# Layer 1 of a diffusion-transformer trunk: the latent heads' key, query and value projections moved into the unit loops of neighbourhood and latent attention

## Chip, cores, metric

One core of one Trainium2 chip runs the whole program. The metric is the device time of one execution in microseconds (us). Engines: PE (TensorE) multiplies matrices and transposes, DVE (VectorE) reduces and does elementwise work, ACT (ScalarE) does exp, squares and copies, POOL (GpSimd) does elementwise work in SBUF, SP (SyncE) issues the DMAs. Each engine works through its own queue in order; semaphores hold an instruction back until its inputs are there, and everything queued behind it on that engine waits too.

## Reference, cut to what matters

Two layers over 512 tokens and 256 context tokens, all in float32. Only the mixer of layer 1 is touched:

```python
def mixer_mla_na(h, hc, row, col, ...):
    cq, ckv, kr, nq, nk, nv = split_cols(h @ w_in, sizes)        # also for hc
    # latent heads: 8 heads, 96 = 64 + 32 rotary columns
    mq = rope_tail(rmsnorm((rmsnorm(cq) @ w_uq).reshape(..., 8, 96)))
    kv = (rmsnorm(ckv) @ w_ukv).reshape(..., 8, 64 + 64)
    mk = rope_tail(rmsnorm(concat(kv[..., :64], kr)));  mv = kv[..., 64:]
    o_mla = block_attention(mq, [mkc, mk], [mvc, mv])             # 768 keys
    # neighbourhood heads: 8 heads of 64; window of 8 x 16 columns plus 256 context keys, with a bias
    o_na = neighbourhood_attention(q_na, k_na, v_na, k_nac, v_nac, rpb)
    out = concat([o_mla, o_na]) @ w_out
```

## The kernel before, in words

A float32 product is made of three matmuls (`mm3`): each operand is kept as a high part H and a remainder L. `unit` loads a weight (`wraw`), ACT casts it to H (`wH`), and DVE or POOL subtracts to get L (`wL`).

Layer 1's mixer runs in four stretches. (1) `run_chunks` projects the hidden state: neighbourhood queries, keys, values, and the normalised latents `cq` (384 wide) and `ck` (256 wide). (2) **Neighbourhood attention**: 4 pairs of heads x 4 blocks of 128 queries = 16 *units*. A unit has `scores` (8 matmuls of 256 columns, then softmax: maximum `mc`, bias with maximum, factor `nb` on DVE, two exponentials on ACT, reciprocal `rs` on DVE, scaling of `prob` on POOL), `turn` (8 transposes of `prob` on PE, copied out as `PT` by ACT or DVE), `values` (16 matmuls into `ps_pv`). (3) **Projections of the latent heads**, a `run_chunks` of its own: keys of heads 0 to 3, queries 0 to 3, values 0 to 3, queries 4 to 7, four heads at a time (`two_tiles`). A *make* is the matmuls of two token tiles, then squares on ACT, their sums `ss` on DVE, a reciprocal root on tiles of eight columns (`rsqrt`: `nwm`, `rq` and three rounds of `nwt`, `nwt`, `rq`, all on DVE), the products `qn` and `qr`, for queries a rotation (three products on POOL, one addition on DVE). A *turn* of heads is then 4 transposes on PE for a pair of heads (`turn_pair`) and H and L copied out (`mQH` on ACT, `mQL` on DVE; for keys `mKH`, `mKL`). (4) **Latent attention**: again 16 units, with 12 score matmuls for two heads over 768 keys, 12 transposes, 24 value matmuls; the keys and values of heads 4 to 7 are spread over its first units as background (`more_heads`, `moreq`).

`paired` sets the order of the units on PE: scores of unit u, then the first two groups of transposes of unit u-1, values of unit u-2, background, the rest of the transposes of u-1. `tc.issue_after` pins each block behind the last PE instruction, so PE's order is the one written. The order on DVE, ACT and POOL is chosen when the program is built and is fixed at run time.

Of the kernel before, what the change touches and what calls it, by code (L numbers as in the profile page):

```python
# [28 lines left out]
MLTAB = False  # L29
MKR = 0.8  # L30
EARLY = 3
TAB1 = False
TABR = True
UQ = 4
WS1, NAPT = 4, 6


class Products:


    def __init__(self, engine):
        self.engine, self.last = engine, None

    def matmul(self, *a, **kw):
        self.last = self.engine.matmul(*a, **kw)  # L45
        return self.last

    def transpose(self, *a, **kw):
        self.last = self.engine.transpose(*a, **kw)  # L49
        return self.last  # L50
# [3 lines left out]
def trunk(ctx: ExitStack, tc: tile.TileContext, A: dict, out: bass.AP):  # L54
    nc = tc.nc
    act, dve, pool, pe, sp = nc.scalar, nc.vector, nc.gpsimd, Products(nc.tensor), nc.sync
# [278 lines left out]

    def rope(dst, src, C, S, half, tmp):
# [4 lines left out]
        later(lambda: dve.tensor_tensor(dst, dst, tmp, op=ALU.add), 1)  # L341
# [67 lines left out]
    def paired(units, fill):  # L409
# [5 lines left out]
        def block(f):  # L415
            with tc.issue_after(pe.last.ins):
                f()
# [12 lines left out]
        while True:  # L430
            unit = next(units, None)
            if unit is None and turned is None and valued is None:
                break
            if unit:
                block(unit[0])
            for f in turned[1][:2] if turned else ():
                block(f)
# [3 lines left out]
            for f in turned[1][2:] if turned else ():  # L441
                block(f)
            unit, turned, valued = None, unit, turned
# [514 lines left out]
    with tc.tile_pool(name="g1", bufs=1, side="left") as gp, tc.tile_pool(name="ws1", bufs=1, side="right") as wp:  # L958

        def na_heads(typ, half, tiles, gain, sink):  # L960
# [5 lines left out]
            def compute(units):  # L966
                for t0 in tiles[::2]:
                    pt = (ps_one if t0 < 4 else ps_pv)([P, 512])
# [71 lines left out]
    def kv_units(g, v):  # L1040
        return [unit(A["wukv"][g][:, 512 * v + 256 * i:512 * v + 256 * i + 256], 256, base, tag="c", bufs=KT) for i in range(2)]

    early = []
    mixs = [None] * 8
    with tc.tile_pool(name="atq", bufs=1, side="left") as aq, tc.tile_pool(name="at1", bufs=1, side="left") as ap:
        def low_queries(pr):

            QB = [aq.tile([P, TM], F32R, tag="nQB" + x, name="nQB" + x, bufs=2) for x in "HL"]
            for a, b in zip(QQ[pr], QB):
                both_halves(a, b)  # L1050
            return QB


        QBs = {pr: low_queries(pr) for pr in range(2)}
        V2 = [slot3(F32, name=f"V2{i}")[:, :512] for i in range(3)]
        for i in range(3):
            sp.dma_start(out=V2[i][0:64], in_=V[i][64:128])
            sp.dma_start(out=V2[i][64:128], in_=V[i + 1][0:64])
        base_col = (0, 8, 24, 32)
        wv = ((V[0], V[1]), (V2[0], V2[1]), (V2[1], V2[2]), (V[2], V[3]))  # L1060

        def na_units(pr):
            mixs[4 + pr] = group_pair(0, "mix")
            if pr == EARLY:
                early.extend([kv_units(0, 0)])
            pvs = {}
            QB = QBs.pop(pr) if pr in QBs else low_queries(pr)

            bias = {}
            for hd in range(2):  # L1070
                for i, b in enumerate((0, 1, 3)):
                    bias[hd, b] = base.tile([P, TC], F32, tag="c" + "HL"[hd], name="bias", bufs=KT)
                    sp.dma_start(out=bias[hd, b], in_=A["bias"][2 * pr + hd, i])
                    pool.tensor_scalar(bias[hd, b], bias[hd, b], 8.0, 1.0, op0=ALU.mult, op1=ALU.mult)
                bias[hd, 2] = bias[hd, 1]
            for b in range(4):
                tq = slice(128 * b, 128 * b + 128)
                st = {}

                def scores(b=b, tq=tq, st=st):  # L1080
                    wk = slice(8 * base_col[b], 8 * base_col[b] + 256)
                    st["p"] = [ap.tile([P, 512], F32, tag="P", name="prob", bufs=5) for _ in range(2)]
                    for hd in range(2):
                        S = ps_one([P, 512])
                        (QH, QL), K = (QQ[pr], QB)[hd], (KA, KB)[hd][pr]
                        for so, ko in ((slice(0, 256), wk), (slice(256, 512), CTX)):
                            pe.matmul(S[:, so], QH[:, tq], K[:, ko], start=True, stop=False)
                            last = pe.matmul(S[:, so], QL[:, tq], K[:, ko], start=False, stop=True)
                        mc = small.tile([P, 2], F32, tag="mc", name="mc")
                        mx = small.tile([P, 2], F32, tag="mx", name="mx")  # L1090
                        dve.reduce_max(mc[:, 0:1], S[:, 256:512], axis=AX)
# [360 lines left out]
```

## Time and profile before

| | |
|---|---|
| three timed runs | median 1741.58 us (1740.38 to 1742.42) |
| the profiled execution | 1739.45 us, span 1737.7 us |
| busy over the span | PE 1655.2 us (95%), DVE 942.6 (54%), ACT 631.0 (36%), POOL 251.8 (14%) |
| chain that ended last | PE 87%, DVE 6%, ACT 3%, POOL 2% |

The span runs from the first to the last instruction; 1.8 us of the execution lie outside it. The profile also gives, for each stretch, the clock that PE was granted as a share of 2.4 GHz (1.2 GHz is 0.5). Matmuls overlap, so that a "busy" PE may still be fed slowly; the spacing of starts tells more.

### The profile page before, as it was taken

Reading aid. Unit: us, or ns where it says so; the run is one execution under the profiler, and the core shown is the slowest. Engines: PE = TensorE matmul, PEld = TensorE weight load, DVE = VectorE, ACT = ScalarE, POOL = GpSimd, SP = SyncE. Lnnn points to the kernel's source line nnn. Section 1 sums busy time; section 2 is a strip of 40 time slices with the busy share of each in tenths; the row PEclk is TensorE's granted clock in tenths of the full one; section 3 lists DMA queues with packets and bytes.
Section 4 is the critical chain, followed back from the end, with each engine's and each line's share of the span. In section 5 each row is a group of like instructions: output and inputs, shape, how many; then the busy total and the mean of one; then the engine's idle time right before and its main releaser. Section 6 shows DMA issues by size and latency. Waiting matters only on the chain.

```text
span 1737.7 us, 28925 instructions
## 1 busy us (share of the span) xinstructions
PE 1655.2 (95%) x11590; PEld 1469.8 (85%) x11590; DVE 942.6 (54%) x2052; ACT 631.0 (36%) x1217; POOL 251.8 (14%) x440
## 2 busy tenths in 40 slices
PE   6898999999999999999999999777999999999999
PEld 3688677788888888888889999666789998999897
DVE  5687567555845524433326874568866633333332
ACT  4454556524221221221224643454554432232221
POOL 1341333211000000000001202455330100000000
PEclk8899999999999999999999999897999999999999
DMA  7401334311635513522212223302003132222221
GB/s 280 156 35 53 137 131 171 131 39 54 210 102 175 171 56 134 170 70 65 70 64 100 79 70 97 91 15 76 25 25 134 40 109 96 85 98 98 98 77 58
DMA packets 60662, 171.23 MB, mean 99 GB/s; under 512 B 7152, under 2 KB 14576, under 8 KB 60528
## 3 DMA queue, kind: packets, MB, share of 16 engines
q1 hardware_dynamic: 60528, 169.39, 29.0%
q8 instruction: 91, 1.49, 0.3%
q14 instruction: 43, 0.35, 0.1%
HBM read 160.05 MB, written 4.19 MB: 95 GB/s over the span
## 4 chain that ended last, share of the span: by engine, by line
PE 87%; DVE 6%; ACT 3%; POOL 2%; DMA 1%; issue 1%; SPq 0%; POOLq 0%; ACTq 0%; DVEq 0%
PE ps_one L45 52%; PE ps_tp L45 15%; PE ps_pv L45 9%; PE ps_big L45 7%; PE ps_tp L49 5%; ACT prob L395 1%; POOL prob L399 1%; DVE mx L390 0%; DVE wL L144 0%; DVE win L648 0%; DVE ss L350 0%; ACT wH L143 0%; DVE rq L269 0%; DVE qn L598 0%; DVE nwt L267 0%
## 5 line engine op out<-in xcount | busy, mean ns | idle before, releaser
L143 ACT CAST wH<-wraw 128x1024 fp32r<-128x1024 f32 (+5 forms) x209 | 194.3, 937 | 390.9 <-PE ps_one L45 209.6
L144 DVE TENSOR_TENSOR wL<-wraw,wH 128x1024 fp32r<-128x1024 f32 (+4 forms) x199 | 222.9, 1125 | 172.2 <-ACT wH L143 170.0
L45 PE MATMUL ps_one<-hH,wL 128*128 128x512 f32 (+1 forms) x704 | 236.8, 336 | 0.0
L45 PE MATMUL ps_one<-hL,wH 128*128 128x512 f32 (+1 forms) x704 | 236.7, 336 | 0.0
L45 PE MATMUL ps_one<-hH,wH 128*128 128x512 f32 (+1 forms) x704 | 236.7, 336 | 0.0
L45 PE MATMUL ps_tp<-hH,wL 128*128 128x256 f32 x704 | 196.6, 280 | 0.0
L45 PE MATMUL ps_tp<-hL,wH 128*128 128x256 f32 x704 | 196.3, 279 | 0.0
L45 PE MATMUL ps_tp<-hH,wH 128*128 128x256 f32 x704 | 196.0, 280 | 0.0
L45 PE MATMUL ps_one<-aH,wL 128*128 128x512 f32 (+1 forms) x560 | 194.0, 347 | 0.0
L45 PE MATMUL ps_one<-aL,wH 128*128 128x512 f32 (+1 forms) x560 | 193.9, 347 | 0.0
L45 PE MATMUL ps_one<-aH,wH 128*128 128x512 f32 (+1 forms) x560 | 193.5, 347 | 0.0
L309 POOL TENSOR_SCALAR hH<-nt 128x256 fp32r<-128x256 f32 (+1 forms) x72 | 39.5, 557 | 736.6 <-ACT nt L308 734.6
L45 PEld LDWEIGHTS ps_one<-hH,wL 128*128 128x128 f32 x704 | 132.2, 188 | 15.4
L45 PEld LDWEIGHTS ps_one<-hL,wH 128*128 128x128 f32 x704 | 132.2, 188 | 14.4
L45 PEld LDWEIGHTS ps_one<-hH,wH 128*128 128x128 f32 x704 | 132.3, 188 | 14.2
L399 POOL TENSOR_SCALAR prob<-prob,rs 128x768 f32<-128x768 f32 (+2 forms) x136 | 105.2, 782 | 195.7 <-DVE rs L397 157.0
L45 PEld LDWEIGHTS ps_tp<-hH,wH 128*128 128x128 f32 x704 | 132.3, 188 | 0.9
L45 PEld LDWEIGHTS ps_tp<-hL,wH 128*128 128x128 f32 x704 | 132.0, 188 | 1.0
L45 PEld LDWEIGHTS ps_tp<-hH,wL 128*128 128x128 f32 x704 | 132.2, 188 | 0.1
L49 PE MATMUL ps_tp<-ident,prob 128*128 128x128 f32 x656 | 99.5, 285 | 20.6 <-POOL prob L399 18.0
L45 PEld LDWEIGHTS ps_one<-aH,wH 128*128 128x128 f32 x560 | 105.8, 189 | 14.7
L45 PEld LDWEIGHTS ps_one<-aL,wH 128*128 128x128 f32 x560 | 105.6, 189 | 14.5
(274 smaller groups left out, 3456.3 us busy)
## 6 DMA issues: line engine op xcount, KB each, us to landing
wraw<-in_ada_dram SPq DMA_DIRECT2D x80, 512.0 KB, 3.7
wraw<-in_wg_dram SPq DMA_DIRECT2D x44, 512.0 KB, 3.5
wraw<-in_wu_dram SPq DMA_DIRECT2D x44, 512.0 KB, 3.5
wraw<-in_wd_dram SPq DMA_DIRECT2D x32, 384.0 KB, 3.1
wraw<-in_wd_dram SPq DMA_DIRECT2D x16, 512.0 KB, 3.5
wraw<-in_w1n_dram SPq DMA_DIRECT2D x12, 512.0 KB, 3.4
adaw<-in_adaq_dram SPq DMA_DIRECT2D x16, 256.0 KB, 5.4
wraw<-in_adaq_dram SPq DMA_DIRECT2D x8, 512.0 KB, 5.6
```

The lines of the kernel that those rows point to most:

```text
L45: self.last = self.engine.matmul(*a, **kw)
L49: self.last = self.engine.transpose(*a, **kw)
L143: act.copy(H, raw[:, :cols])
L144: eng.tensor_tensor(L, raw[:, :cols], H.bitcast(F32), op=ALU.subtract)
L309: last = (pool.tensor_scalar(H, t[:, :n], 1.0, 1.0, op0=ALU.mult, op1=ALU.mult), sub(L, t[:, :n], H))
L395: act.activation(pr[i], S[:, i, :], AF.Exp, bias=nb[:, i:i + 1], scale=scale, accum_out=sm[:, i:i + 1])
L399: pool.tensor_scalar(pr[i], pr[i], r[:, i:i + 1], 1.0, op0=ALU.mult, op1=ALU.mult)
```

## The change

Stretch (3) is gone. Its makes and turns become small closures that are listed, unit by unit, in `na_plan` and `mla_plan`; `paired` runs the closures of a unit between the values and the transposes. Both attentions are one sequence of 32 units on the same score, probability and `PT` buffers, with no drain between them. Queries are made two heads at a time (192 columns instead of 384), so there are 8 query makes instead of 4, each with its own reciprocal root. In neighbourhood units the softmax of both heads is joint (one `mc`, one `nb`, one `rs`), and all transposes of a unit come after values and background (0 early groups, 2 before). The zero rows of queries and keys are written once per buffer over all tokens. The `wL` of the key and value weights moves from DVE to POOL, and the addition of the rotation stands right behind its products.

```diff
+    def padded(pair):
+        for x in pair:
+            pool.memset(x[96:128, :].bitcast(F32), 0.0)
+        return pair
...
+    def query_steps(pr, w):
...
+        def make(t0):
+            if t0 == 0:
+                mQ[2 * pr:2 * pr + 2] = [padded(group_pair(0, "mQ") if pr < 2 else mQx[2 * pr - 4 + i]) for i in range(2)]
+                st["w"] = w()
+            pt = ps_pv([P, 2, 256])
+            for i in range(2):
+                tok_gemm(pt[:, i, :192], st["w"], 1, 192, lq[t0 + i])
+            o = st[t0] = raw_heads(2)
+            hv = pt[:, :, :192].rearrange("p t (h d) -> p t h d", d=96)
+            r = tile_rstd(hv, o)
...
+            dve.tensor_tensor(qn, hv[..., 64:96], bc(r, [P, 2, 2, 32], 3), op=ALU.mult)
+            dve.tensor_tensor(o[..., 0:64], hv[..., 0:64], bc(r, [P, 2, 2, 64], 3), op=ALU.mult)
...
+            rope(o[..., 64:96], qn, C, S, 16, tmp, now=True)
+
+        def turn(t0):
+            turn_pair(t0, st[t0], gcol["mqg"], mQ[2 * pr:2 * pr + 2])
+
+        return [f for t0 in (0, 2) for f in ((lambda t0=t0: make(t0)), (lambda t0=t0: turn(t0)))]
...
             background()
-            for f in turned[1][2:] if turned else ():
+            for f in unit[4] if unit else ():
                 block(f)
-            unit, turned, valued = None, unit, turned
+            for f in turned[1][early:] if turned else ():
+                block(f)
+            turned, valued = unit, turned
...
+                dve.reduce_max(mc, S[:, :, 256:512], axis=AX)
...
+                softmax(S, 2, 512, 0.125, st["p"], mx)
...
+    na_plan = [q[0][:1], q[0][1:2], q[0][2:3], q[0][3:], q[1][:1], q[1][1:2], q[1][2:3], q[1][3:],
+               keys0[0][:1], keys0[0][1:2], turns0[0][:1], keys0[0][2:], turns0[0][1:2], turns0[0][2:] + [v0], [], []]
+    mla_plan = [vals0[:2], vals0[2:] + turns0[1][:1] + [hq[0]], turns0[1][1:] + [k1], q[2][:1],
+                q[2][1:2] + keys1[0][:1], q[2][2:3] + turns1[0][:1], q[2][3:] + keys1[0][1:2] + [v1, hq[1]], keys1[0][2:] + turns1[0][1:],
+                vals1[:2], vals1[2:] + q[3][:1], q[3][1:3] + turns1[1][:1], q[3][3:] + turns1[1][1:],
+                [], [], [], []]
...
-        paired((u for pr in range(4) for u in mla_units(pr)), [(moreq, 2 * MKR)])
+    uq0()
+    k0()
+    paired(both_attentions())
```

On DVE, a neighbourhood unit before had its two heads one after the other, and the next unit's maxima between them (`mc`: maximum over the context scores; ISA: bias and maximum; `rs`: reciprocal of the exponentials' sum):

```order
L1091 TENSOR_REDUCE mc<-ps_one 128x1
L1092 ISA ps_one,mx<-ps_one,bias,mc 128x256
L1092 ISA mx 128x1
L1091 TENSOR_REDUCE mc<-ps_one 128x1
L392 TENSOR_SCALAR nb<-mx 128x1
L1092 ISA ps_one,mx<-ps_one,bias,mc 128x256
L1092 ISA mx 128x1
L392 TENSOR_SCALAR nb<-mx 128x1
L144 TENSOR_TENSOR wL<-wraw,wH 128x256
L397 RECIPROCAL rs<-sm 128x1
L1091 TENSOR_REDUCE mc<-ps_one 128x1 x2
```

In the change, with a query make (here the first) beside units 0 and 1, the same engine has:

```order
L375 TENSOR_SCALAR nb<-mx 128x2
L380 RECIPROCAL rs<-sm 128x2
L1090 TENSOR_REDUCE ss<-qr 128x4
L238 TENSOR_SCALAR nwm<-ss 128x4
L244 TENSOR_SCALAR rq<-nwm 128x4
L247 SCALAR_TENSOR_TENSOR nwt<-rq 128x4
L1212 TENSOR_REDUCE mc<-ps_big 128x2
...
L1143 TENSOR_TENSOR qn<-ps_pv,rq 128x128
L1144 TENSOR_TENSOR qr<-ps_pv,rq 128x4x64
L380 RECIPROCAL rs<-sm 128x2
L322 TENSOR_TENSOR qr<-qr,rt 128x4x32
L345 SCALAR_TENSOR_TENSOR mQL<-ps_tp,par,mQH 96x256 x2
```

`rs` of the even unit now stands directly behind its `nb`, the make's sums behind that, the odd unit's maximum behind these, and the rotation's addition (L322) behind the odd unit's `rs`.

On PE, the block between two units' scores of the neighbourhood loop was transposes and values alone; in the change the first turn of queries (L1080) stands behind the scores of unit 1 and ahead of the transposes of unit 0's probabilities:

```order
L1211 MATMUL ps_big<-nKB,nQBL 128x256
L1080 MATMUL ps_tp<-ident,qr 96x128 x4
L389 MATMUL ps_tp<-ident,prob 128x128 x8
L1210 MATMUL ps_big<-nKA,nQH_9220 128x256
```

The make of these queries stands one unit earlier. In the latent loop (unit 4) the turn stands behind the values and ahead of a key make and of unit 3's last transposes:

```order
L1270 MATMUL ps_pv<-PT,mV_9195 64x128 x2
L1080 MATMUL ps_tp<-ident,qr 96x128 x4
L135 MATMUL ps_pv<-wH,ck_9201 128x256
L136 MATMUL ps_pv<-wL,ck_9201 128x256
L137 MATMUL ps_pv<-wH,ck_9202 128x256
...
L389 MATMUL ps_tp<-ident,prob 128x128 x4
L135 MATMUL ps_big<-mKH,mQH 128x512
```

Before, these transposes belonged to stretch (3), where no attention unit was queued behind them.

## Rows read from the trace of the kernel before

**Rows 1.** The page, part 2: PE busy and granted clock, 40 slices, in tenths.
```profile
PE   6898999999999999999999999777999999999999
PEclk8899999999999999999999999897999999999999
```
**Rows 2.** Windows: the four stretches; busy us (count) by engine, PE clock, DMA.
```profile
1089.20:1163.20 74.00, 56.34 (x512) 47.03 (x512) 43.80 (x179) 39.05 (x94) 33.62 (x73) 0.93 0.20 51
1163.20:1213.90 50.70, 35.58 (x206) 33.06 (x203) 40.92 (x135) 22.69 (x53) 32.27 (x90) 0.79 0.21 71
1213.90:1267.90 54.00, 50.20 (x422) 44.00 (x421) 41.41 (x114) 29.67 (x65) 15.28 (x21) 0.97 0.12 38
1267.90:1315.00 47.10, 46.64 (x456) 40.50 (x454) 29.16 (x67) 24.43 (x52) 15.97 (x18) 1.00 0.01 4
```
**Rows 3.** Timeline of PE, a neighbourhood unit without stalls (start, us, instruction).
```profile
1108.20 0.39 PE L45 MATMUL ps_one<-nKA,nQH 128*128 128x256 f32 x1
...
1109.25 1.03 PE L49 MATMUL ps_tp<-ident,prob 128*128 128x128 f32 x8
...
1111.24 0.39 PE L45 MATMUL ps_one<-nKA,nQH 128*128 128x256 f32 x1
```
**Rows 4.** Timeline of PE: the first work after three gaps (gap in brackets).
```profile
1095.57 1.11 PE L49 MATMUL ps_tp<-ident,prob 128*128 128x128 f32 x4 [4.35 <-POOL prob L399]
1124.72 1.92 PE L49 MATMUL ps_tp<-ident,prob 128*128 128x128 f32 x8 [2.80 <-POOL prob L399]
1190.66 0.69 PE L45 MATMUL ps_big<-wH,cq 128*128 128x384 f32 x1 [3.94 <-DVE qr L1167]
```
**Rows 5.** Groups by form, 1087 to 1320 us: softmax and rotation (busy us, mean ns).
```profile
L1092 DVE CUSTOM_DVE_ANT_0 ps_one<-ps_one,bias,mc 128x256 f32<-128x256 f32 x32 | 15.2, 485 | 0.3
L395 ACT ACTIVATE prob<-ps_one,nb 128x512 f32<-128x512 f32 x32 | 21.8, 688 | 7.5 <-DVE nb L392 7.3
L395 ACT ACTIVATION_READ_ACCUMULATOR prob<-ps_one,nb 128x1 f32 x32 | 6.4, 201 | 0.0
L399 POOL TENSOR_SCALAR prob<-prob,rs 128x512 f32<-128x512 f32 x32 | 21.9, 692 | 21.9 <-DVE rs L397 11.1 <-PE ps_one L45 4.9 <-DVE nb L392 4.2
L340 POOL TENSOR_TENSOR qr<-qn,tab1q 128x128 f32<-128x128 f32 x8 | 3.7, 467 | 0.0
```
**Rows 6.** Groups by form on DVE, 1164 to 1214 us: makes and turns.
```profile
L1149 DVE TENSOR_REDUCE ss<-qr 128x8 f32<-128x512 f32 x3 | 2.1, 688 | 2.4 <-ACT qr L1147 2.4
L267 DVE SCALAR_TENSOR_TENSOR nwt<-rq 128x8 f32<-128x8 f32 x21 | 5.8, 284 | 0.3
L268 DVE TENSOR_TENSOR nwt<-nwt,nwm 128x8 f32<-128x8 f32 x21 | 3.8, 187 | 0.4
L269 DVE SCALAR_TENSOR_TENSOR rq<-nwt,rq 128x8 f32<-128x8 f32 x21 | 5.0, 246 | 0.4
L362 DVE SCALAR_TENSOR_TENSOR mQL<-ps_tp,par,mQH 96x256 fp32r<-96x256 f32 x12 | 5.5, 474 | 0.2
```
**Rows 7.** Timeline, latent unit 2 beside a key make: PE's scores, PE's next turn, DVE's sums and last root step.
```profile
1227.84 0.48 PE L45 MATMUL ps_big<-mKH,mQH 128*128 128x512 f32 x1
...
1232.47 0.64 PE L49 MATMUL ps_tp<-ident,qr 128*96 128x128 f32 x4
...
1228.73 0.68 DVE L1149 TENSOR_REDUCE ss<-qr 128x8 f32<-128x512 f32 x1
...
1235.08 0.17 DVE L269 SCALAR_TENSOR_TENSOR rq<-nwt,rq 128x8 f32<-128x8 f32 x1
```
**Rows 8.** Timeline of PE: a key make up to its turn, and two latent units without background.
```profile
1246.09 0.39 PE L45 MATMUL ps_pv<-wH,ck 128*128 128x256 f32 x1
...
1247.61 0.60 PE L49 MATMUL ps_tp<-ident,qr 128*96 128x128 f32 x4
...
1273.11 0.48 PE L45 MATMUL ps_big<-mKH,mQH 128*128 128x512 f32 x1
...
1278.13 0.47 PE L45 MATMUL ps_big<-mKH,mQH 128*128 128x512 f32 x1
```

More of the change, by code (lines that the diff above doesn't have):

```diff
@@ L407, in transposed, with paired @@
         copy_out(dst, tp[:, :128 * n].rearrange("p (a b) -> p a b", a=n), acts, of)
-    def paired(units, fill):
+    def paired(units, fill=()):
         debt = [0.0] * len(fill)
         def block(f):
-            with tc.issue_after(pe.last.ins):
+            last = next(i for i in reversed(nc.cur_bb.bb.instructions) if i.engine == mybir.EngineType.PE)
+            with tc.issue_after(last):
                 f()
@@ new lines, in value_steps, with make, once, get @@
+    def value_steps(g, w):
+        def make(t0):
+            pt = ps_pv([P, 2, 256])
+            for i in range(2):
+                tok_gemm(pt[:, i, :], w(), 1, 256, lk[t0 + i])
+            for i in range(2):
+                act.copy(mV[t0 + i][:, 256 * g:256 * g + 256], pt[:, i, :])
+        return [lambda t0=t0: make(t0) for t0 in (0, 2, 4)]
+    def once(f):
+        got = []
+        def get():
+            if not got:
+                got.append(f())
+            return got[0]
+        return get
@@ new lines, in trunk, with mla_units, scores, turn @@
+    wo1 = [[]]
+    def mla_units(pr, plan):
+        pvs = {}
+        if pr == 3:
+            for i in range(4):
+                wo1[0] += cut(unit(A["w1o"][0][:, 256 * i:256 * i + 256], 256, base, tag="c", bufs=KT, eng=pool), 2)
+        for t in range(4):
+            tq = slice(128 * t, 128 * t + 128)
+            st = {}
+            def scores(tq=tq, st=st):
+                st["p"] = [ap.tile([P, TT], F32, tag="P", name="prob", bufs=4) for _ in range(2)]
+                for hd in range(2):
+                    (QH, QL), (KH, KL_) = mQ[2 * pr + hd], mK[2 * pr + hd]
+                    S = ps_big([P, 1024])
+                    for ko in (MAIN, CTX):
+                        mm3(S[:, ko], (QH[:, tq], QL[:, tq]), (KH[:, ko], KL_[:, ko]), True, True)
+                    softmax(S[:, :TT].unsqueeze(1), 1, TT, 96 ** -0.5, [st["p"][hd]])
+            def turn(i, st=st):
+                if i == 0:
+                    st["t"] = ap.tile([P, 12, 128], F32, tag="PT", name="PT", bufs=2)
+                transposed([st["p"][j // 6][:, 128 * (j % 6):128 * (j % 6) + 128] for j in range(4 * i, 4 * i + 4)],
+                           st["t"][:, 4 * i:4 * i + 4, :])
+            def values(t=t, tq=tq, st=st):
+                if t == 0:
+                    pvs["pv"] = ps_pv([P, 512])
+                for kt in range(6):
+                    for hd in range(2):
+                        h = 2 * pr + hd
+                        pe.matmul(pvs["pv"][64 * hd:64 * hd + 64, tq], mV[kt][:, 64 * h:64 * h + 64],
+                                  st["t"][:, 6 * hd + kt, :], start=kt == 0, stop=kt == 5)
+                if t == 3:
+                    mixs[pr] = group_pair(0, "mix")
+                    put_pair(pvs["pv"], 512, mixs[pr])
+            yield scores, [lambda i=i, turn=turn: turn(i) for i in range(3)], values, 2, plan[t]
@@ new lines, in both_attentions @@
+    def both_attentions():
+        nonlocal mKx, mQx
+        for pr in range(4):
+            yield from na_units(pr, na_plan[4 * pr:4 * pr + 4])
+        wqs.close()
+        aqs.close()
+        na.close()
+        mp = mla.enter_context(tc.tile_pool(name="mla", bufs=1, side="left"))
+        mQx = [tuple(mp.tile([P, TM], F32R, tag=f"mQ{x}{i}", name=f"mQ{x}{i}") for x in "HL") for i in range(4)]
+        mKx = [mp.tile([P, TT], F32R, tag=f"mKx{i}", name=f"mKx{i}") for i in range(4)]
+        for pr in range(4):
+            yield from mla_units(pr, mla_plan[4 * pr:4 * pr + 4])
```

334 lines of the change are left out of this document (130 added, 204 removed).

## The prediction, made before the changed kernel was timed

> **What bounds the kernel now.** I read the page's slices first [rows 1]. PE is busy nine tenths or more nearly everywhere; only slices 26 to 28 show 7, and there the granted clock falls too. That is layer 1's mixer, so I cut it into its stretches with the windows view [rows 2]: 74.0 us neighbourhood attention, 50.7 us projections of the latent heads, 54.0 us latent attention with background and 47.1 us without, 225.8 us in all. PE is busy 56.3 of 74.0 and 35.6 of 50.7 us in the first two, against 50.2 of 54.0 and 46.6 of 47.1 in the others. At the same time DVE is busy 40.9 of 50.7 us in the projections (81%) and 43.8 of 74.0 (59%) in neighbourhood attention. So two engines matter: PE has 38 us without work in the whole, DVE has 70.
>
> Then the timeline. A neighbourhood unit without stalls takes PE 3.04 us [rows 3], so that 16 take 48.7 of the 74 us. A latent unit without background takes 5.02 us [rows 8], 16 take 80.3. A key make takes 1.52 us [rows 8]; its turn half a microsecond. With 6 key and 6 value makes, queries worth about 16 us and 20 turns, PE's work in the 225.8 us is about 173 us at full clock. Moving the projections into the units could therefore gain up to 50 us, if nothing but PE counted. What decides is whether DVE can deliver each make in the time that PE needs to come to its turn.
>
> **The change, part by part.** *Query units of neighbourhood attention (units 0 to 7).* A make and its turn stand in alternate units. I lay out two units from the end of an even unit's scores, in DVE's order as shown with the change. The joint maximum over 2 x 256 costs what a sum over 512 costs, 0.69 [rows 6]; two bias passes at 0.485 [rows 5], their accumulators and `nb` bring it to 2.0 us. Two exponentials with their accumulator, 2 x 0.69 + 0.2 less a small overlap [rows 5], end at 3.5. `rs` waits for both, and DVE has nothing ahead of it: 1.5 us idle. Then `ss` (0.55 for 384 elements, between nothing and the 0.69), the odd unit's maximum after its scores, bias and `nb` with the first root steps in between: 7.9. PE has meanwhile done values 1.0, the next make 2.0, transposes 1.0, scores 1.05 and values 1.0, and has nothing left from 6.9. The remaining five root steps at some 0.2 [rows 6], `qn` and `qr` end at 9.6; the rotation's three POOL products, each at most 0.47 [rows 5], end at 10.45, its addition at 10.8. Only now the turn can start; the 8 transposes of the even unit and the next scores are queued behind it on PE. Turn 0.5, transposes 1.0, scores 1.05: 13.4 us for two units, with a stall of 4 us in it. Before, two units took 2 x 74.0/16 = 9.25.
>
> The first pair takes longer, about 19: the query weights' `wL` and eight new zero fills stand on POOL ahead of the first probabilities, and PE waits for the weights. The zero fills (32 x 512 and 32 x 768) have no row; I bound one by nothing and by a whole `prob` pass of 0.69 [rows 5], 0 to 5.5 us for eight, and take half, which the first softmax mostly hides; with no cover it is 3 us. The 192-column matmul has no row either: between nothing and the 0.127 us of a key make's twelve [rows 8], 0 to 2.3 us a make; I take 2.0, near the upper row, the nearest there is. So units 0 to 7 take 19 + 3 x 13.4 = 59 us at full clock.
>
> *Units 8 to 15* carry three key makes and three turns, the last two nothing. A key turn comes two units after its make, so PE does not wait for it; DVE sets the pace. Its work is 8 x 2.4 for softmax and `PT`, 3 x 3.6 for makes (sums, nine root steps at 0.24 [rows 6], products), 6 x 0.47 for `mKL` [rows 6], 0.7 for the mix: 33.5, and some 1 us a unit waiting for exponentials in the units that have nothing to fill it: 39 us.
>
> *Latent units.* PE's work is 80.3 + 4 query makes x 2.0 + 9 key or value makes x 1.5 + 13 turns x 0.5 = 108. Here the trace shows the chain itself [rows 7]: scores start at 1227.84, the make's sums at 1228.73, and its last root step, threaded between two heads' maxima, ends at 1235.25, 7.4 us after the scores began. Less one `mKL` that stood in between, that is 7.0; with `qn`, the rotation and its addition, 8.75 us after the scores began. PE comes to the turn 4.63 us after them (1232.47, [rows 7]). Before, that was the turn of an earlier make; now it is this one's, so PE waits 4.1 us. This holds for units 4, 6 and 10. In unit 11 the sums start earlier: 2.7. In unit 7 a key make is followed by its own turn: squares, sums, nine steps and product, 5.0. With 1 us for unit 5 the stalls are 21 us, and the latent units take 129 us against 101.1 before.
>
> *What a stall costs besides.* After gaps of 2.8 to 4.35 us PE runs at its lower level, 1.2 GHz: eight transposes took 1.92 us at 1124.72 [rows 4] against 1.03 [rows 3], and the first 384-column matmul after 3.94 us took 0.69 [rows 4]; stretch 3 had a mean clock of 0.79 [rows 2]. Behind each new stall stand a turn, transposes and scores, 2.5 us of PE work that would double. Eight stalls cost 0 to 20 us; I take 9, since a slower PE also finds DVE further ahead. The Trainium skill (TensorE: Matmul & The Clock Gate, section "HAM oscillation — how this bites in real kernels") says that waits between groups of matmuls can send the clock back to its lower level group after group, so that each begins slow; by that the whole 20 would be paid, and [rows 4] agree for the gaps named.
>
> *Free parts.* `wL` on POOL: POOL is busy 33.6 of 74 us [rows 2], and the units that get them have spare POOL time. Later queue positions of DMAs on SP: DMA engines are 20% busy there [rows 2]; uncovered, one late weight is one transfer of some 3 us. The boundary without drain saves about 2 us of waiting, which is in the sum, since I count units straight through.
>
> **Sum.** First scores 1.0; units 0 to 7 59 + 4 of the clock's 9; units 8 to 15 39; latent units 129 + 5; less 2.1, since units 0 to 15 were counted to the end of unit 16's scores: 235 us against 225.8. That is +9 on the profiled execution's 1739.45, so 1748.5; the runs' median stands 2.1 above that execution. I forecast **1749 us**. Ends: query units 54 to 70, the next 35 to 41, latent 120 to 142: 209 to 252 us, -17 to +26, hence 1724 to 1767.
>
> **Rivals.**
> *Faster.* The turn's chain on DVE is shorter than I lay it out, because softmax work and root steps fill each other's gaps, and PE comes to the turns when they are ready. For it: DVE has 70 us without work in the stretch, and held 81% through stretch 3 [rows 2]. Its work grows by four roots, 4 x 9 x 0.24 = 8.6, to 164 us; at 81% that takes 202, a gain of 23: 1718; halfway between that and no change, 1730. Against it: order on DVE is fixed, and [rows 7] show 7 us. It decides at latent unit 4: a wait under 2 us there means this case.
> *No change.* PE fills neighbourhood attention's gaps and gives the same back at the turns: eight stalls of 2.5 instead of 4 us take 12 off the sum and leave 223: 1739. The change then moves the idle time and does not shorten it.
> *Clock in full.* Every stall pays the lower level, +11: 1760. Stretch 3 ran so; against it, PE is fed better between the stalls here.
>
> **How the numbers follow.** Forecast (own range 1745 to 1757) 0.43, faster 0.31, no change 0.20, clock in full 0.06. A difference of 0.2%, 3.5 us, is about what a measurement of this kernel can tell from none. So slower 0.49, same 0.20, faster 0.31. The range takes in most of the faster case and the upper bound: 1722 to 1764.
>
> **What would show it.** In the profile after: stretch 3 gone; eight neighbourhood units in about 60 us, where before eight took 37; waits of PE of some 4 us at the turn of queries, released by DVE's or ACT's work on `qr`; PE clock below 0.95 through the first 100 us; DVE near 75% busy. Wrong would be: PE's longest waits at the turns under 2 us, or no waits but a clock near 1.

## The result and the profile after

The changed kernel takes 1798.91 us (median of 4 runs, 1798.47 to 1800.78) against 1741.66 of the kernel before on the same chips: ratio 1.0332, interval [1.0314, 1.0349]. It is slower by 57 us. Forecast were 1749 and a range of 1722 to 1764: the sign was right, the size was not. All the time is lost in layer 1's mixer: from the first scores of neighbourhood attention to the first feed-forward matmul behind it the trace of before has 272.3 us (1089.2 to 1361.5), that of after 331.1 (1089.3 to 1420.4).

The page of after, part 2, against [rows 1]:

```profile
PE   6897999999999999999999996678679999999999
PEclk8898999999999999999999997799889999999999
```

Windows of after: units 0 to 7, units 8 to 15, latent units 0 to 11, each from scores to scores (us; busy us and count of PE, its weight loads, DVE, ACT, POOL; clock, DMA share, GB/s).

```profile
1089.26:1162.81 73.55, 44.20 (x306) 39.42 (x305) 37.11 (x130) 25.56 (x59) 27.81 (x52) 0.72 0.20 51
1162.81:1208.70 45.89, 35.70 (x306) 31.06 (x305) 31.72 (x111) 22.05 (x55) 18.38 (x31) 0.89 0.05 15
1208.70:1341.37 132.67, 98.78 (x792) 87.67 (x790) 77.49 (x222) 57.26 (x127) 44.45 (x69) 0.89 0.10 31
```

The low stretch has not gone, as a kernel without stretch 3 should show: it has grown from three slices to six. In units 0 to 7 PE works 44 of 73.6 us, at a clock of 0.72, and no other engine is busy for more than 37.1. That is the picture of a chain of waits, not of a full engine. Lines of the view of waits, after, 1089 to 1366 us, name it (us in total, times, longest):

```profile
PE ps_tp L1080 <- DVE qr L322: 40.3, 8, 6.3
PE ps_tp L389 <- ACT PT L165: 6.0, 5, 2.9
PE ps_pv L135 <- DVE qr L1111: 5.4, 3, 3.3
PE ps_tp L1080 <- POOL qr L1113: 5.0, 1, 5.0
DVE qr L322 <- POOL qr L320: 9.0, 8, 2.0
```

All eight query turns (L1080) wait for the rotation's addition (L322), 5.0 us in the mean; unit 7's key turn waits as long. One of them in order of time, units 2 and 3 (start, us, instruction, idle time before):

```profile
1111.57 0.36 PE L135 MATMUL ps_pv<-wH,cq 128*128 128x192 f32 x1
...
1114.45 0.55 DVE L1090 TENSOR_REDUCE ss<-qr 128x4 f32<-128x384 f32 x1 [0.56 <-ACT qr L1087]
1114.91 1.37 POOL L382 TENSOR_SCALAR prob<-prob,rs 128x512 f32<-128x512 f32 x2
1115.04 0.60 DVE L238 TENSOR_SCALAR nwm<-ss 128x4 f32<-128x4 f32 x1
...
1116.42 0.69 DVE L1212 TENSOR_REDUCE mc<-ps_big 128x2 f32<-128x512 f32 x1
...
1119.58 0.41 DVE L1144 TENSOR_TENSOR qr<-ps_pv,rq 128x256 f32<-128x256 f32 x1
...
1120.85 0.78 DVE L322 TENSOR_TENSOR qr<-qr,rt 128x128 f32<-128x128 f32 x1 [0.60 <-POOL qr L320]
1121.77 1.06 PE L1080 MATMUL ps_tp<-ident,qr 128*96 128x128 f32 x4 [5.11 <-DVE qr L322]
...
1124.60 1.09 PE L389 MATMUL ps_tp<-ident,prob 128*128 128x128 f32 x4 [0.91 <-DVE PT L167]
```

The make starts at 1111.57, its sums at 1114.45; the next unit's maximum (1116.42) stands between its root steps, the product starts at 1119.58, the rotated half is there at 1121.6, and PE, out of work at 1116.7, begins the turn at 1121.77. Then turn, transposes and scores run at the lower clock level: the turn took 1.06 us against 0.60 in [rows 8]. The window from this turn to the end of unit 4's scores, in the columns of the windows above:

```profile
1121.77:1127.38 5.61, 4.70 (x22) 4.08 (x23) 1.50 (x3) 1.53 (x3) 1.22 (x3) 0.50 0.05 18
```

The granted clock was 0.50 (1.2 GHz) in all of it. In the 2.5 us behind each of the eight query turns it was 0.50 seven times and 0.57 once. In the two pairs with the longest waits (6.27 and 6.14 us, units 5 and 7) POOL adds to the chain: it scales both heads' probabilities first, though `qn` is ready. Unit 5:

```profile
1137.12 0.27 DVE L1143 TENSOR_TENSOR qn<-ps_pv,rq 128x128 f32<-128x128 f32 x1
1137.37 1.36 POOL L382 TENSOR_SCALAR prob<-prob,rs 128x512 f32<-128x512 f32 x2 [3.92 <-DVE rs L380]
1138.69 0.32 POOL L318 TENSOR_TENSOR rt<-qn,tab1q 128x64 f32<-128x64 f32 x1
```

### The profile page after: what moved, and what is told of

It reads as the page before. It is cut to its first block, busy times and chain, and to the rows that moved or that the text cites. A ratio compares the mean times of both kernels' runs of the same rounds, so it can differ in the third digit from the quotient of the medians.

```text
span 1796.7 us, 29025 instructions
## 1 busy us (share of the span) xinstructions
PE 1674.8 (93%) x11662; PEld 1488.7 (83%) x11662; DVE 949.9 (53%) x2052; ACT 633.7 (35%) x1224; POOL 256.1 (14%) x403
## 4 chain that ended last, share of the span: by engine, by line
PE 84%; DVE 7%; ACT 3%; POOL 2%; issue 1%; DMA 1%; SPq 0%; ACTq 0%; POOLq 0%; DVEq 0%
PE ps_one L136 16%; PE ps_one L135 16%; PE ps_one L137 16%; PE ps_tp L137 5%; PE ps_tp L135 5%; PE ps_tp L136 5%; PE ps_tp L389 4%; PE ps_pv L777 2%; PE ps_pv L135 2%; PE ps_pv L136 1%; PE ps_pv L137 1%; PE ps_big L135 1%; PE ps_big L136 1%; PE ps_big L137 1%; ACT prob L378 1%
## 5 line engine op out<-in xcount | busy, mean ns | idle before, releaser
L123 ACT CAST wH<-wraw 128x1024 fp32r<-128x1024 f32 (+6 forms) x212 | 194.4, 926 | 393.0 <-PE ps_one L136 194.5
L124 DVE TENSOR_TENSOR wL<-wraw,wH 128x1024 fp32r<-128x1024 f32 (+3 forms) x191 | 219.6, 1155 | 169.2 <-ACT wH L123 167.3
L378 ACT ACTIVATE prob<-ps_big,nb 128x768 f32<-128x768 f32 (+2 forms) x136 | 104.5, 775 | 48.1 <-DVE nb L375 33.2
L135 PEld LDWEIGHTS ps_one<-aH,wH 128*128 128x128 f32 x560 | 105.8, 189 | 14.7
```

Source lines behind the costliest of these rows:

```text
L123: act.copy(H, raw[:, :cols])
L124: eng.tensor_tensor(L, raw[:, :cols], H.bitcast(F32), op=ALU.subtract)
L135: pe.matmul(o, aH, bH, start=first, stop=False)
L378: act.activation(pr[i], S[:, i, :], AF.Exp, bias=nb[:, i:i + 1], scale=scale, accum_out=sm[:, i:i + 1])
```

## The experiments

The theory (own make): a query turn stands one unit behind its make, the make's chain over ACT, DVE and POOL is longer than PE's work up to the turn, and everything behind the turn in PE's queue waits with it. Rivals: the new form of neighbourhood attention's softmax (both heads at once) makes the units long; the half clock behind the waits; POOL's zero fills; the number of PSUM buffers; DVE's total work. Times are medians, ratios are to the kernel before, timed beside each run. The split by stretches stands in a table behind the ninth run; it is that of the one profiled execution of each kernel.

**Run 1: turns two units behind their makes in neighbourhood attention.**

```diff
-    na_plan = [q[0][:1], q[0][1:2], q[0][2:3], q[0][3:], q[1][:1], q[1][1:2], ...
+    na_plan = [q[0][:1], q[0][2:3], q[0][1:2], q[0][3:], q[1][:1], q[1][2:3], ...
```

> One change to the kernel after: in the eight units of neighbourhood attention that carry queries, each turn stands two units behind its make (make, make, turn, turn) instead of one. Own-make theory (a query turn waits on PE for the DVE chain of a make that is one unit old, and everything behind it on PE waits too): the four waits there of 5.1 to 6.3 us, 22.9 in sum, and the half clock behind them go; units 0 to 7 fall from 73.6 to about 50 us and the whole from 1799 to about 1775. Softmax-form theory (the joint softmax of two heads with all transposes behind the background makes the units long): the units keep 65 us or more and the whole stays above 1790.

Measured: 1785.34 us, 1.0264 [1.0246, 1.0282]. Units 0 to 7 fell from 73.6 to 55.2 us, as the own-make theory has it and the softmax theory does not; but units 8 to 15 rose from 45.9 to 52.8, so that 13.6 us remain of the 24 expected. Two of the four waits are left, 3.5 and 3.6 us at units 3 and 7.

**Run 2: the same in the latent units too.**

```diff
-  ... turns0[1][1:] + [k1], q[2][:1], q[2][1:2] + keys1[0][:1], q[2][2:3] + turns1[0][:1], ...
+  ... turns0[1][1:] + [k1] + q[2][:1], keys1[0][:1], q[2][1:2] + q[2][2:3], keys1[0][1:2] + turns1[0][:1], ...
```

> As the run before, and in the latent units too every query turn and unit 7's key turn stand at least two units behind their make. Own-make theory: the latent waits at query turns (17.3 us), at unit 7's key turn (5.0) and at its make (3.3) go as well, with the half clock behind them (about 10): some 30 us less than the run before, about 1743, near the kernel before. Softmax-form theory: latent units were not changed in form, so the latent part may gain, but the neighbourhood part stays above 110 us for its 16 units, and the whole above 1765.

Measured: 1775.47 us, 1.0201 [1.0184, 1.0218]. The latent units 0 to 11 gave 12.5 of the 30 us expected. PE's waits in this run, 1089 to 1343 us, show why:

```profile
PE ps_pv L135 <- DVE qr L1144: 7.8, 3, 2.8
PE ps_pv L135 <- DVE qr L1111: 7.5, 3, 2.9
PE ps_tp L1080 <- DVE qr L322: 7.2, 3, 3.5
PE ps_tp L389 <- POOL prob L382: 6.0, 1, 6.0
```

The turns' waits fell from 40.3 to 7.2 us, but in their place the next make now waits for the product of the make ahead of it (L1144 and L1111, 15.3 us): of the two `ps_pv` buffers the values' accumulator holds one, and each make keeps the other until the end of its chain. And a wait of 6.0 us for POOL is new. So the own-make wait is a true cause, and the PSUM wait stood behind it; where the wait for POOL comes from, run 3 shows.

**Run 3: PE computes through the wait.**

```diff
         tp = ps_tp([P, 2, 256])
+        for _ in range(fill):
+            pe.matmul(tp.rearrange("p a b -> p (a b)"), ckH[:, 0, 0:128], ckH[:, 0, 0:512], start=True, stop=True)
```

`fill` is 16 for query turns and 0 for key turns.

> The kernel after, with 16 matmuls of 512 columns on data that is always there, written into the query turn's own result tile ahead of its transposes (they are overwritten), so that PE computes through its wait. Some 3.8 us of matmuls at full clock, for a wait of 4 to 6 us. Clock theory (a good part of the loss is the half clock after each wait): eight turns with 2.5 us each of work that no longer doubles, 15 to 25 us less, 1775 to 1785. Own-make theory alone, with the clock as a small part: within 6 us of 1799, since the chain on DVE is as long as before.

Measured: 1796.22 us, 1.0321 [1.0305, 1.0336]; 2.7 us less than after, with intervals that overlap. Yet units 0 to 7 took 66.0 us instead of 73.6, at a mean clock of 0.90 instead of 0.72, and units 8 to 15 took 7.2 us more, with one wait of 6.75 us in them. Behind unit 3's turn the clock was back:

```profile
1119.91:1124.00 4.09, 3.21 (x32) 2.88 (x34) 2.09 (x4) 1.50 (x3) 1.31 (x3) 1.00 0.13 37
```

The clock theory holds locally, 7.5 us for four waits in these units and 3 in the latent ones, about half of what it expected, and the whole does not show it, because something else took it back. It is on POOL. First after, then this run (the last row is PE's):

```profile
1205.19 1.36 POOL L382 TENSOR_SCALAR prob<-prob,rs 128x512 f32<-128x512 f32 x2 [2.08 <-DVE rs L380]
...
1207.29 0.73 POOL L1067 MEMSET mKL<- 32x768 f32 x1
```

```profile
1199.16 0.73 POOL L1067 MEMSET mKL<- 32x768 f32 x1 [1.80 <-PE ps_big L1213]
...
1204.27 2.77 POOL L1067 MEMSET mKx<- 32x768 f32 x4
1207.14 1.36 POOL L382 TENSOR_SCALAR prob<-prob,rs 128x512 f32<-128x512 f32 x2
...
1207.89 1.97 PE L389 MATMUL ps_tp<-ident,prob 128*128 128x128 f32 x8 [6.75 <-POOL prob L382]
```

In after the last neighbourhood unit's probabilities stand ahead of the zero fills of the latent queries and keys on POOL; in this run the build has put them behind the fills, 8 us of them, and PE waits. The same wait, 6.0 to 8.0 us, stands in runs 1 to 4, 8 and 9: in each run that keeps the fills. So each of these six has a cost in units 8 to 15 that comes from POOL's order and not from what it tests.

**Run 4: background behind the transposes of the unit before** (in `paired`, the two loops that issue `unit[4]` and the remaining transposes change places).

> The kernel after, with a unit's background issued behind the transposes of the unit before instead of ahead of them; plan and distances of turns as they are. Own-make theory: each turn comes on PE one block of eight transposes later (1 to 2 us), so eight waits of 5 shrink by that much and the probabilities' transposes no longer stand behind them, 10 to 20 us less: 1780 to 1790. If it were not the place of the turn in PE's queue that counts but DVE's total work: no change, 1797 to 1801. Against a gain: makes come later too, and DVE gets their sums later, which could give all of it back.

Measured: 1797.90 us, 1.0330 [1.0304, 1.0355]. Units 0 to 7 gave 7.0 us, units 8 to 15 took 6.0 back with the fills' wait (8.0 us here). In the whole, no change, which is the number of the rival. The step expected is not what gave the 7.0 us: the four turn waits of units 0 to 7 hardly shrank, 21.7 us against 22.9.

**Runs 5 and 6: no zero fills, on after and on run 2.**

```diff
-        for x in pair:
-            pool.memset(x[96:128, :].bitcast(F32), 0.0)
...
-                        mm3(S[:, ko], (QH[:, tq], QL[:, tq]), (KH[:, ko], KL_[:, ko]), True, True)
+                        mm3(S[:, ko], (QH[:96, tq], QL[:96, tq]), (KH[:96, ko], KL_[:96, ko]), True, True)
```

> The kernel after without POOL's 32 zero fills of rows 96 to 127: the latent scores contract over the 96 rows that hold data instead of 128, with the same result. Zero-fill theory (the fills, 0.52 to 0.73 us each and 20 us in all, stand in POOL's queue ahead of the probabilities' passes and of the keys' products): at least 8 us less, 1791 or below, most of it in the first two units and at units 14 to 17. Own-make theory: PE's waits at the query turns end with DVE's addition and not with POOL's fills, so within 4 us of 1799.

> The same edit on top of the run with all turns late (1775.5), where PE waited 6.0 us for the last neighbourhood unit's probabilities while POOL worked through twelve fills. Zero-fill theory: that wait falls under 2 us and units 14 to 17 give 6 to 10 us with the clock, 1765 to 1770. If the fills only stand where POOL would wait for something else anyway: 1773 to 1777.

Measured: 1801.53 us, 1.0345 [1.0325, 1.0365] on after, so the fills cost after nothing; 1769.10 us, 1.0155 [1.0131, 1.0178] on run 2, 6.4 us less, as the zero-fill theory has it: units 0 to 7 from 54.5 to 47.7 and units 8 to 15 from 52.7 to 47.1, while the latent units 0 to 11 took 4.7 more. The fills are a cost in waiting: hidden as long as something slower stands ahead, and paid as soon as that is removed.

**Run 7: makes copy their product out of PSUM at once, on run 6.**

```diff
+            act.copy(o, hv)
...
-            dve.tensor_tensor(o[..., 0:64], hv[..., 0:64], bc(r, [P, 2, 2, 64], 3), op=ALU.mult)
+            dve.tensor_tensor(o[..., 0:64], o[..., 0:64], bc(r, [P, 2, 2, 64], 3), op=ALU.mult)
```

The edit also moves `qn` and `rt`, which had one buffer each, into the tile of their make; no run separates the two.

> On top of the run before: each query and key make copies its product from PSUM to SBUF on ACT at once and DVE takes the products from that copy, so that the PSUM buffer comes free after two ACT operations and not with the last product of the chain, some 8 us later. PSUM theory (of two buffers the values hold one, so a make cannot begin before the make ahead of it has gone through its whole chain on DVE; with late turns this wait took the turn's place, 15.3 us in six waits): the six waits go, the latent units 3 to 11 fall from about 10 to about 8 us each, 15 to 22 us less than the run before. Rival, DVE's order sets the pace (a unit with a make and a turn has 8 us of work on DVE plus waits for exponentials): PE then waits elsewhere, for the turns again, and less than 6 us are gained.

Measured: 1747.86 us, 1.0034 [1.0023, 1.0045]: 21 us less than run 6, at the upper end of the PSUM theory. The latent units 0 to 11 fell from 123.7 to 104.0 us, and waits of PE for L1144 and L1111 at `ps_pv` are gone. The Trainium skill (Perfetto Trace Analysis, section "Optimization Strategy") says that the same gap coming back on the engine that should be full can mean too few buffers for the next tile. Run 2's six waits of 2.3 to 2.9 us are such gaps, and run 7 bears it out.

**Run 8: neighbourhood attention's softmax head by head, on after.**

```diff
-                dve.reduce_max(mc, S[:, :, 256:512], axis=AX)
...
-                softmax(S, 2, 512, 0.125, st["p"], mx)
+                for hd in range(2):
+                    dve.reduce_max(mc[:, hd:hd + 1], S[:, hd, 256:512], axis=AX)
...
+                    softmax(S[:, hd:hd + 1, :], 1, 512, 0.125, [st["p"][hd]], mx[:, hd:hd + 1])
```

> The kernel after with one part undone: neighbourhood attention's softmax head by head (maximum, bias pass, exponential and division of one head after the other, as before the change) in place of both heads together; all else as in after. Softmax-form theory: each of the 16 units has its first exponential 1.2 us earlier and is 0.5 to 1 us shorter, 1785 to 1791. Own-make theory: two more small operations a unit on DVE stand in the chain of the make, so no gain, 1797 to 1805.

Measured: 1802.16 us, 1.0349 [1.0324, 1.0373]. Units 0 to 7 took 74.3 us against 73.6, so there is no gain there. Units 8 to 15 took 50.4 against 45.9 with the fills' wait in them (7.6 us), so that this run can't tell for them; run 16 does.

**Run 9: run 7's copy alone, on after.**

> The kernel after with the early copy from PSUM alone; turns one unit behind their makes and the zero fills as in after. If the two causes stand in a row (first the turn waits for its own make, and only with that gone does the next make wait for the PSUM buffer): PE still waits 4 to 6 us at eight query turns, the buffer is not what ends these waits, and little is gained, 1792 to 1801. If the buffer alone were the cause and the late turns only moved work: 1775 or less.

Measured: 1812.30 us, 1.0404 [1.0388, 1.0420]; 13 us slower than after, beyond both expectations. PE's waits, 1085 to 1380 us:

```profile
PE ps_tp L1080 <- DVE qr L322: 42.5, 8, 7.2
PE ps_tp L1080 <- POOL qr L1115: 11.2, 3, 4.8
PE ps_tp L389 <- POOL prob L382: 6.1, 1, 6.1
```

With the turns still behind their own makes, the copy does not shorten their waits: the eight query waits are 42.5 us against 40.3, the longest 7.2 against 6.3, as a copy ahead of the squares on ACT would have it. Units 0 to 7 took 76.5 us, 2.9 more. The larger part of the 13 us is not the copy's own: units 8 to 15 took 53.6, 7.7 more, with the fills' wait (6.1 us) in them. The edit that gave 21 us as the third step gave nothing as the first.

Where the runs spend their time, us from scores to scores (last column: from latent unit 12's scores to the first feed-forward matmul):

| kernel | units 0-7 | units 8-15 | latent 0-11 | rest |
|---|---|---|---|---|
| after | 73.6 | 45.9 | 132.7 | 79.0 |
| run 1, late turns, neighbourhood | 55.2 | 52.8 | 131.5 | 78.9 |
| run 2, late turns | 54.5 | 52.7 | 119.0 | 80.8 |
| run 3, PE kept busy | 66.0 | 53.1 | 129.7 | 78.9 |
| run 6, + no fills | 47.7 | 47.1 | 123.7 | 80.0 |
| run 7, + PSUM free early | 49.3 | 46.6 | 104.0 | 80.9 |
| run 15, below | 46.3 | 44.0 | 108.0 | 75.1 |
| run 18, below | 47.0 | 42.5 | 104.2 | 77.2 |

Before had 199.0 us in what corresponds to the first three columns together, stretch 3 included, and 73.3 in the last. The last column differs by up to 2.9 us between runs 15 to 18, whose edits do not touch that part: from the output projection's first matmul to the first feed-forward one the clock was 1.00 in runs 15 and 17, 0.94 in 16 and 0.97 in 18.

**Run 10: latent makes spread further, on run 7** (another `mla_plan`: `keys1[0][:2]` in unit 3, `keys1[0][2:]` in unit 5, `q[3][:1]` in unit 7).

> On top of the run of 1747.9 with late turns, no fills and early copies: in the latent units the makes move forward so that no turn stands next to or right behind its make (the last key make one unit earlier, the last two query makes two and one earlier). Own-make theory: PE's remaining waits at unit 7's key turn (3.9 us) and at unit 11's (3.4, behind two further turns) go, with the half clock behind them: 6 to 10 us less, 1738 to 1742. Rival, DVE's total work in these units is the bound: within 3 us of 1747.9.

Measured: 1758.91 us, 1.0092 [1.0078, 1.0105]; 11 us slower than run 7, beyond both expectations. Unit 7 took 19.3 us. In it, in order of time:

```profile
1247.23 8.49 SPq L116 DMA_DIRECT2D wraw<-in_wuq_dram  x3
1250.84 0.35 ACT L123 CAST wH<-wraw 128x192 fp32r<-128x192 f32 x1
...
1254.74 0.53 PE L135 MATMUL ps_pv<-wH,cq 128*128 128x192 f32 x1 [1.80 <-ACT wH L123]
...
1257.73 0.53 PE L135 MATMUL ps_pv<-wH,cq 128*128 128x192 f32 x1 [1.57 <-ACT wH L123]
```

The last query weights arrive one by one while their make runs. They are loaded through the same four buffers that hold the makes' heads, and three of these were taken by keys that were not turned yet.

**Runs 11 and 12: the projection's weight casts behind the last exponentials, then run 4's order too, both on run 10.**

```diff
-                    ws.append(wo_unit(layer, m, wp, nb))
+                    with tc.issue_after(exps[-1].ins):
+                        ws.append(wo_unit(layer, m, wp, nb))
```

> On top of the run before: the output projection's weight casts on ACT (four of 0.97 us, which in after and in all runs so far stand ahead of the last unit's two exponentials) are issued behind these exponentials. Tail theory: PE's wait of 3.3 us between the last scores and the output projection goes, 3 to 4 us less than the run before. Rival: the weights come later by as much, and PE waits for them in place of the exponentials: no change.

> On top of the run before: a unit's background behind the transposes of the unit before, as was tried on after alone, where it changed nothing. Queue theory: with the long waits gone, transposes no longer stand behind turns that are not ready, 3 to 8 us less. Against it: the makes are now what fills the time in which PE would wait for the probabilities in neighbourhood attention; issued behind the transposes they fill nothing, and the 16 neighbourhood units get longer by 0.5 to 1 us each, 8 to 16 us more.

The reason for run 11, in run 7's last unit (after has the same casts and the same wait):

```profile
1306.57 3.89 ACT L123 CAST wH<-wraw 128x1024 fp32r<-128x1024 f32 x4 [1.32 <-PE ps_big L137]
1307.45 0.14 DVE L375 TENSOR_SCALAR nb<-mx 128x1 f32<-128x1 f32 x1
...
1310.84 0.90 ACT L378 ACTIVATE prob<-ps_big,nb 128x768 f32<-128x768 f32 x1
...
1312.77 0.58 PE L135 MATMUL ps_one<-mixH,wH 128*128 128x256 f32 x1 [3.31 <-ACT prob L378]
```

`nb` is ready at 1307.6, the exponential starts at 1310.8 behind four casts. Measured in run 11: 1757.57 us, 1.0084 [1.0071, 1.0097]; the wait fell from 3.31 to 0.46 us and the projection started 2.9 us sooner after the last scores, but only 1.3 us came through, since PE then waited 2.0 us at the last unit's values. Run 12: 1749.60 us, 1.0043 [1.0029, 1.0056], 8 us less than run 11, units 0 to 15 from 96.2 to 90.5 us. The same order that did nothing on after now gives what it was expected to.

**Runs 13 to 15: both edits on run 7; on a plan that loads the last query weights three units ahead; and all of it together.**

> The run of 1747.9 (late turns, no fills, early copies, latent plan as there) with the projection's casts behind the last exponentials and the background behind the transposes. From the two runs that had these edits on the other plan: 1.3 to 3 us for the casts, 8 for the order, so 1737 to 1741. If the gain of the order belonged to the other plan's late weights alone: 1744 or more.

> The run with casts late (1757.6) with another latent plan: turns stand as far behind their makes as there, but the last query weights are loaded three units ahead of their use and at a time when two of the four shared buffers are free, and the last key turns come earlier so that they give their buffers back. Buffer theory (the three loads, 2.8 us apart through one free buffer, held PE in unit 7, which took 19.3 us): unit 7 falls to 9 us or less, 8 to 14 us less in all, 1744 to 1750. Rival, DVE's total work bounds these units: the time moves to the next units, 1754 or more.

> As the run before, with the background behind the transposes: 4 to 8 us less than it, 1737 to 1744, and with the clock back in more of the stretch perhaps below the kernel before (1741.6). If the makes are needed to fill neighbourhood attention's waits for probabilities: no gain.

Measured: 1742.92 us, 1.0015 [1.0005, 1.0025]; 1746.97, 1.0039 [1.0026, 1.0052]; 1740.14, 0.9997 [0.9986, 1.0008]. Run 13 came out between its two expectations: units 0 to 15 gave 5.6 us and the part behind unit 12 gave 3.7, but the latent units 0 to 11 took 3.4 back. Run 14 is 10.6 us below run 11, as the buffer theory has it: unit 7 took 9.4 us, though unit 6 now takes 14.7. Run 15 is level with the kernel before.

**Runs 16 to 18: on run 15, the softmax by head; that with a buffer of its own for the last key make and a plan that spreads the last makes and turns; that buffer and plan alone.**

```diff
-            o = st[t0] = raw_heads(4)
+            o = st[t0] = raw_heads(4) if g == 0 or t0 < 4 else kh[0].tile([P, 768], F32, tag="kh", bufs=1)
```

> The run of 1740.1 with neighbourhood attention's softmax head by head. Softmax-form theory, now that the turns' waits are gone: POOL has the first head's probabilities about 1 us earlier, the seven waits of PE for them (7.7 us) shrink to half, 3 to 5 us less, 1735 to 1737. If more small operations on DVE cost what the earlier start gives, as in after: 1739 to 1744.

> As the run before, and the last key make of the latent units writes its heads into a buffer of its own, the last query weights are loaded one unit earlier and the last query makes and key turns spread over units 7 to 11. Buffer theory: units 7 to 9 (13.0, 9.9 and 11.5 us in the run of 1740.1) lose 4 to 8 us together. Rival, DVE's total work: within 3 us of the run before.

> The run of 1740.1 with that buffer and spread alone, softmax for both heads together: 4 to 8 us less than 1740.1 by the buffer theory, within 3 us by the rival.

Measured: 1745.66 us, 1.0013 [1.0004, 1.0022]; 1740.32, 0.9987 [0.9978, 0.9997]; 1739.26, 0.9981 [0.9971, 0.9991]. The softmax by head gains nothing here, with no fills in the way: units 0 to 15 took 91.6 us against 90.3. Buffer and plan give 0.26% with it (intervals apart; 5.3 us, as the buffer theory has it) and 0.16% without (intervals that overlap; 0.9 us, as the rival has it). The units named in the expectation (6 to 8, counted from 0) lost 5.3 us in run 17 and 0.6 in run 18; in the first three columns the two gave 3.5 and 4.6 us, so which theory holds stays open. Runs 17 and 18 are ahead of both kernels, by up to 0.2% and by 0.1 to 0.3% of the kernel before, about the least that can be told. Run 18's clock in the mixer is back, as part 2 of its page shows:

```profile
PE   6898999999999999999999999779899999999999
PEclk8899999999999999999999999999999999999999
```

## Why the prediction was right in its sign and wrong in its size

The mechanism it named is there: the turn waits for its own make (runs 1 and 2), at eight turns, released by the chain's last operation, with the lower clock behind each. What failed is the size it gave to that chain and to what stands behind a stall, and the waits of the latent units that it left out. The error of 50 us comes apart into these terms, by the windows above.

- **The tail, 8 us, a slip in the sum.** Sixteen latent units were counted at 5.02 us, scores to scores, but behind the last scores stand the transposes and values of two units. Before has 26.8 us from unit 12's scores (the line below) to the end of the stretch in [rows 2]; the sum, with its terms for the boundaries, had 19.

```profile
1288.18 0.47 PE L45 MATMUL ps_big<-mKx,mQH 128*128 128x512 f32 x1
```

- **Units 0 to 7: forecast 59 + 4, measured 73.6, 10.5 us.** The first two units took 18.7 us (19 forecast). The other pairs took 17.4, 18.3 and 19.2 instead of 13.4. Counted from the end of the even unit's scores, PE was out of work after 6.5 to 7.7 us (6.9 forecast) and began the turn after 11.8, 12.8 and 13.9 (10.8 forecast). The layout had nothing on POOL between `qn` and the rotation, and POOL's passes stood there in the last two pairs (1.3 us each); and in the first and last of the three, small operations on DVE took longer beside POOL (1.4 and 1.0 us in sum). From the turn to the end of the next scores it was 5.3 to 5.6 us instead of 2.55: 4.5 to 4.8 us of PE work at a clock of 0.50, and a wait of 0.8 to 0.9 for a copy of `PT`. The sum had 4 of the clock's 9 for the four stalls.
- **Units 8 to 15: forecast 39, measured 45.9, 6.9 us.** DVE was busy 31.7 us (33.5 forecast); what was too small is its idle time between. PE's nine waits there over 0.25 us add up to 10.1, the longest 2.9 for a copy of `PT`. No run brought these units under 42 us, and which wait sets them stays open. The fewer `PT` and score buffers that both attentions now share were never undone alone.
- **Latent units 0 to 11: forecast 109 + 5 (129 + 5 less four units), measured 132.7, 18.7 us.** The stalls forecast were of the right kind and size: units 4, 6 and 10 waited 4.35, 3.92 and 4.34 us (4.1 forecast), unit 7's key turn 5.0 (5.0), unit 11 4.7 (2.7), unit 5 1.35 (1). Missing were the waits beside them, about 10 us: unit 7's make waited 3.3 for the PSUM buffer, unit 11's turns another 1.6, and smaller ones; PE was without work for 33.9 us instead of 21. The other 6 us are PE's busy time, 98.8 us against 88 + 5: the clock, 0.89 in the mean, and the transposes and values of the last neighbourhood units, which no term held. No run tells these two apart.
- **From unit 12's scores to the first feed-forward matmul, 5.7 us (73.3 before, 79.0 after), had no term.** 2.9 us of it are the casts ahead of the last exponentials; the sum had no row for ACT's order there. Unit 12 itself took 5.9 us instead of 5.0, beginning at the lower clock, and the output projection 1.8 more, at a clock of 0.97 against 1.00.

Three small slips in the working matter little: PE has 37 us without work in [rows 2], not 38; the 2.1 us between the runs' median and the profiled execution were named and not added, which would have made 1750.6; and the ends, 1724 to 1767, are not quite the range given.

"Clock in full" (1760) was closest among the rivals, and its premise is what the rows show: the clock was at or near 0.50 behind each of the eight turns. The Trainium skill's rule (TensorE: Matmul & The Clock Gate, section "HAM oscillation — how this bites in real kernels"), that waits between groups of matmuls can send the clock back group after group, agrees with that. Its price explains little of the error: 4.5 to 4.8 us of PE work at 0.50 cost some 2.3 us a turn more than at 1.00, an estimate of 18 us for eight, and run 3 got back 10.5, against the 9 that the sum took. The zero fills, which the sum bounded at the first pair alone, were hidden in after and cost 6 us once the turns no longer hid them. "Faster" was to be decided by the wait at latent unit 4, under 2 us; it was 4.35. Its ground, DVE's total work, falls too: the forecast sign "DVE near 75% busy" did not come (50, 69 and 58% in the three windows of after), and run 18 has DVE busy for 165.6 us in a mixer of 225.5 us, after 169.8 in 288.2. PE's 37 us without work were hardly filled by any version: run 18's mixer takes as long as that of before (225.8), with PE idle for 34. The lower bound of 54 for the query units was passed only with late turns and no fills (46 to 50).

What the prediction lacked is the row of causes: own make, then the PSUM buffer and the fills, which the turns had hidden. The weight buffers came with the plan of run 10, and the casts' wait of 3.3 us stood openly in after. So single edits on after gave between -23.4 us (all turns late) and +13.4, and late turns, no fills and early copies in a row gave 51.

## What to carry to other kernels

Work moved into the gaps of another stage needs a distance from make to use that is longer than its chain in that company, and buffers for every make on the way: count both before counting the gaps. Where several waits stand in a row, the removal of one tells little of the others; look at what PE waits for next, and go on. An edit also reshuffles the order on the other engines, so a cost that was hidden (fills, casts) can surface without having been touched: read their queues at the seams again after each.

## What was not expected of the hardware

Small operations on DVE took longer beside POOL. In after `nwm` on 128x4 took 0.60 us while POOL scaled probabilities (1115.04, above) and 0.71 beside a zero fill, and 0.16 to 0.17 in the other six makes; the rotation's addition took 0.77 to 0.98 in three of eight, each with a pass on POOL begun just before it, and 0.29 in the other five. At 1115.04 `nwm` and the step behind it ended at 1115.64 and 1116.31, and POOL's two passes at 1114.91 took 1.37 us, to 1116.28. The Trainium skill (SBUF — State Buffer, section "🔬 SBUF: two separate sides") has it that DVE and GpSimd share a pair of ports that one of them holds for a whole instruction, where the DVE instruction runs in a 2-port mode or has two inputs in SBUF; the addition has two. The rows fit that, and no run here was made to test it.

Scores contracted over 96 rows cost PE what those over 128 cost: the last latent units stand 5.02 to 5.03 us apart in run 6 (96 rows), and 5.02 to 5.03 in before and 5.05 to 5.13 in after (128 rows), all at full clock.
